# Score matmuls over 64 and over 128 rows: zeros under the lo queries

## The chip, the cores and the metric

The kernel runs on one core of one Trainium2 chip. The metric is the device time of one execution in microseconds. Before the change it is 826.6 us, the median of three runs (825.56 to 832.39).

## The reference, cut to what matters

A trunk of two decoder layers over 512 tokens of width 1024, in float32. Layer 0 is a recurrent time mixing (RWKV-7), layer 1 a causal differential attention over keys and values that are projected once from the result of layer 0. Only the attention touches the change:

```python
s = jnp.einsum('bhcqd,bhckd->bhcqk', q_blk.astype(f32), kf)     # 8 heads, 2 maps, 64 dims a map
s = jnp.where(k_pos[None, :] <= q_pos[:, None], s, -1e30)
prob = jax.nn.softmax(s, axis=-1)
attn = prob[:, :, 0] - lam * prob[:, :, 1]
return jnp.einsum('bhqk,bhkv->bhqv', attn, vf)
```

Each head has two maps (c = 0, 1) with queries and keys of 64 dims of their own; the two softmaxes are subtracted and one product with the values follows. The result is normalised, gated, projected, normalised again and added to the residual, and each layer ends with a gated embedding of its own.

## The kernel before, in words

**Exact products from pairs.** A float32 operand is held as two float32r parts, hi and lo (lo is what hi leaves over). A product is the sum hi·hi + hi·lo + lo·hi. The dense layers do this with three matmuls in a row into one PSUM bank, written by the helper `mm3` (lines 284, 285, 286), each with 128 rows of contraction and mostly 512 columns.

**The scores.** A query or key of one map has only 64 dims, so hi and lo of the keys share one tile: `kF[hg, x]` (loaded in `keys_in`) has the hi dims in rows 0 to 63 and the lo dims in rows 64 to 127. The queries come as two tiles a unit (`queries`, lines 1683 to 1700): `qh` holds the hi queries twice, in both halves of the rows, so one matmul over 128 rows gives hi·hi + hi·lo (line 1730). `ql` holds the lo queries in rows 0 to 63 alone, and a second matmul over 64 rows against the upper half of the keys adds lo·hi to the same bank (line 1731). `MAPS` (line 1611) is the pair of slices 0:64 and 64:128.

**Units, heads, streams.** A unit is one half of the heads (`hg`, four heads) by one block of 128 queries (`qb`); there are eight, in the order hg 0 with qb 0 to 3, then hg 1. A unit with block qb sees (qb + 1) · 128 keys, so its scores are 128, 256, 384 or 512 columns wide. Two generators, `heads_(0)` and `heads_(1)` (lines 1702 to 1774), go through the units with two heads each. A head issues: four score matmuls (two maps, hi and lo; a *group* in what follows); mask and maximum of each map on VectorE (1735, 1739); exponentials with sums on ScalarE (1742); reciprocal, weight and difference of the maps on VectorE (1747, 1749, 1751); one transpose per key block on TensorE (1757); the copy out of PSUM on ScalarE (1762); the products with the values on TensorE (1766). `unit_end` (1776 to 1814) normalises, gates and transposes a finished unit and frees its query tiles; its power runs on GpSimd in the helper `rsqrt` (280).

**What fills the rest of the stage.** The projections of keys, values, queries and gate (`layer1_proj`) run on TensorE in between, as do the first ones of the output projection. The weights come in by SyncE's DMA queue and are split into hi and lo on ScalarE, VectorE and GpSimd (`w_split`, lines 303 to 326; 269, 317, 321, 323).

**The order.** The instruction order of TensorE, VectorE, ScalarE and GpSimd is fixed when the kernel is built. The class `Streams` (lines 59 to 177) is a planner: every stream of work is a generator that yields steps such as `"PE", 0.68` (engine and cost in us), and the planner always issues the step that can start first by its own clocks. A step whose name ends in "!" books its engine, but its own stream goes on without waiting for it. Tiles come from pools by count (`"take"`, `"free"`); `"R"` is the big ring of 42 tiles of 4 KB a row, and both query tiles come from it. `queries` asks for a unit's two tiles as soon as the unit two places earlier has begun. The planner books a pair of score matmuls at 2 · max(0.11, n / 2250) us for n columns. The queries are loaded by three DMAs a unit on ScalarE's queue: hi into both halves of `qh` (line 1696, twice) and lo into `ql` (line 1698), 256 KB each.

Of the kernel before, what the change touches and what calls it, by code (L numbers as in the profile page):

```python
# [8 lines left out]
F32 = mybir.dt.float32  # L9
F32R = mybir.dt.float32r  # L10
# [5 lines left out]
P = 128  # L16
# [185 lines left out]
def yoco_kernel(ctx: ExitStack, tc: tile.TileContext, I, out):  # L202
    nc = tc.nc
# [26 lines left out]
    def bank(tag):  # L230
        return T(pp, [P, 512], "p", bufs=8)

    def R(shape, dt=F32):
        return T(ring, shape, "R", dt, bufs=N_R)

    def HT(shape, dt=F32):
        return T(hp, shape, "H", dt, bufs=N_H)
# [1373 lines left out]
    MAPS = (slice(0, 64), slice(64, P))  # L1611
# [69 lines left out]
    Q_ = {}  # L1681

    def queries(hg):

        for e in range(4):
            yield "wait", ("b", hg, e)
        for qb in range(NB):
            n = units.index((hg, qb))
            if n >= 2:
                yield "wait", ("unit",) + units[n - 2]  # L1690
            yield "take", "R", 2
            qh, ql = Q_[hg, qb] = R([P, 8, P], F32R), R([P, 8, P], F32R)[MAPS[0]]
            hi, lo = (qkD["b"][hg, n, :, :, qb * P : (qb + 1) * P] for n in range(2))
            yield "ACT", 0.9
            for m in range(2):
                nc.scalar.dma_start(qh[MAPS[m]].bitcast(F32), hi)
            yield "ACT", 0.45
            nc.scalar.dma_start(ql.bitcast(F32), lo)
            yield "DMA", 2.5
            yield "set", ("q", hg, qb)  # L1700

    def heads_(par):
        yield "wait", ("lam",)
        for hg, qb in units:
            n = (qb + 1) * P
            if par == 0:
                yield "take", "pw", 1
                U_[hg, qb] = (bank("pw"), T(lp, [P, 4, 2], "rc", bufs=2), T(lp, [P, 4], "oss", bufs=2))
                yield "spawn", unit_end(hg, qb), UEP
                yield "set", ("unit", hg, qb)  # L1710
            yield "wait", ("unit", hg, qb)
            for tb in range(qb + 1):
                yield "wait", ("vT", hg, tb)
            yield "wait", ("q", hg, qb)
            po, rc, oss = U_[hg, qb]
            qh, ql = Q_[hg, qb]
            for x in (par, par + 2):
                yield "wait", ("k", hg, x)
                yield "take", "H", 2
                E = [HT([P, S]) for _ in range(2)]  # L1720
                mx = T(lp, [P, 2], "mx", bufs=4)
                sm = T(lp, [P, 2], "sm", bufs=4)
                c1 = T(lp, [P, 1], "c1", bufs=4)
                scs = []
                yield "take", "pw", 2
                for m in range(2):
                    s_ = bank("pw")
                    yield "PE", 2 * max(0.11, n / 2250)
                    kt = kF[hg, x][:, m, 0:n]
                    nc.tensor.matmul(s_[:, 0:n], qh[:, 2 * x + m, :], kt, start=True, stop=False)  # L1730
                    nc.tensor.matmul(s_[:, 0:n], ql[:, 2 * x + m, :], kt[MAPS[0]], start=False, stop=True)  # L1731
                    scs.append(s_)
                for m in range(2):
                    yield "DVE!" if m == 0 else "DVE", 0.1 + n / 960
                    nc.vector.tensor_tensor_reduce(  # L1735
                        scs[m][:, 0:n], scs[m][:, 0:n], cmask[:, S - n : S], 1.0, -3.0e38, ALU.add, ALU.max, mx[:, m : m + 1]
                    )
                yield "DVE", 0.08
                nc.vector.tensor_scalar(mx, mx, -0.125, None, ALU.mult)  # L1739
                for m in range(2):  # L1740
                    yield "ACT", 0.18 + n / 960
                    nc.scalar.activation(  # L1742
                        E[m][:, 0:n], scs[m][:, 0:n], AF.Exp, bias=mx[:, m : m + 1], scale=0.125, accum_out=sm[:, m : m + 1]
                    )
                    yield "free", "pw", 1
                yield "DVE", 0.1
                nc.vector.reciprocal(rc[:, x, :], sm)
                yield "DVE", 0.13
                nc.vector.scalar_tensor_tensor(c1, sm[:, 0:1], nlam, rc[:, x, 1:2], ALU.mult, ALU.mult)
                yield "DVE+", 0.13 + n / 960  # L1750
                nc.vector.scalar_tensor_tensor(E[0][:, 0:n], E[1][:, 0:n], c1, E[0][:, 0:n], ALU.mult, ALU.add)
                yield "free", "H", 1
                yield "take", "pw", 1
                pt = bank("pw")
                yield "PE", 0.11 * (qb + 1)
                for kb in range(qb + 1):
                    nc.tensor.transpose(pt[:, kb * P : (kb + 1) * P], E[0][:, kb * P : (kb + 1) * P], ident)  # L1757
                yield "free", "H", 1
                yield "take", "H", 1
                aT = HT([P, S])  # L1760
                yield "ACT", 0.06 + n / 1200
                nc.scalar.copy(aT[:, 0:n], pt[:, 0:n])
                yield "free", "pw", 1
                yield "PE", 0.22 * (qb + 1)
                for kb in range(qb + 1):
                    nc.tensor.matmul(  # L1766
                        po[:, x * P : (x + 1) * P],
                        aT[:, kb * P : (kb + 1) * P],
                        vT[hg, kb // 2][:, kb % 2, x * P : (x + 1) * P],
                        start=(kb == 0),  # L1770
                        stop=(kb == qb),
                    )
                yield "free", "H", 1
                yield "set", ("pv", hg, qb, x)

    def unit_end(hg, qb):
        po, rc, oss = U_[hg, qb]
        for x in range(4):
            yield "wait", ("pv", hg, qb, x)
            yield "take", "H", 1  # L1780
            junk = HT([P, P])
            yield "ACT", 0.37
            nc.scalar.activation(
                junk, po[:, x * P : (x + 1) * P], AF.Square, scale=rc[:, x, 0:1], accum_out=oss[:, x : x + 1]
            )
            yield "free", "H", 1
        r = yield from rsqrt(lp, oss, 1.0 / P, SUBLN_EPS, 4, "or")
        yield "DVE", 0.1
        nc.vector.tensor_mul(r, r, rc[:, :, 0])
        yield "wait", ("gT", hg, qb)  # L1790
        yield "take", "R", 1
        oF[qb, hg] = o = R([P, 2, 4, P], F32R)
        yield "take", "H", 1
        og = HT([P, S])
        g_ = gT[hg, qb // 2][:, qb % 2, :]
        yield "DVE", 1.1
        for x in range(4):
            xs = slice(x * P, (x + 1) * P)
            nc.vector.scalar_tensor_tensor(og[:, xs], po[:, xs], r[:, x : x + 1], g_[:, xs], ALU.mult, ALU.mult)
        yield "free", "pw", 1  # L1800
        yield "take", "pw", 1
        pt = bank("pw")
        yield "PE", 0.45
        for x in range(4):
            nc.tensor.transpose(pt[:, x * P : (x + 1) * P], og[:, x * P : (x + 1) * P], ident)
        yield "free", "H", 1
        pv = pt.rearrange("p (a b) -> p a b", b=P)
        yield "ACT", 0.57
        nc.scalar.activation(o[:, 0], pv, AF.Copy, scale=subl)
        yield "DVE", 0.66  # L1810
        nc.vector.scalar_tensor_tensor(o[:, 1], pv, subl, o[:, 0].bitcast(F32), ALU.mult, ALU.subtract)
        yield "free", "pw", 1
        yield "free", "R", 2
        yield "set", ("oF", qb, hg)
# [28 lines left out]
    for hg in range(2):  # L1843
        sc.add(keys_in(hg), QP)
        sc.add(queries(hg), QP)
    for par in range(2):
        sc.add(heads_(par), HDP[par])
# [114 lines left out]
```

## Time and profile before

| | |
|---|---|
| runs | 825.56, 826.6, 832.39 us (median 826.6) |
| profiled execution | 824.56 us, of which the span of the core is 822.8 us |
| mean granted TensorE clock | 0.988 |
| TensorE (PE) busy | 779.5 us, 95% |
| weight loads (PEld) busy | 609.9 us, 74% |
| VectorE (DVE) busy | 595.2 us, 72% |
| ScalarE (ACT) busy | 454.8 us, 55% |
| GpSimd (POOL) busy | 192.6 us, 23% |
| HBM traffic | 144.60 MB by DMA, 176 GB/s on average |

How to read the rows that follow. In a timeline a row is: start in us from the beginning of the span, duration, engine, line, operation, out <- in, and for a matmul the size of the weights (rows * columns), then the moving operand (rows x columns) and the count. Matmuls are pipelined and their ends are modelled, so two rows may overlap: the pace of TensorE is the distance from one start to the next. In a table of windows each engine has its busy time with the number of instructions behind it; then come the granted clock, the share of DMA and GB/s. In a row of groups, the busy time and the mean in ns stand ahead of the idle time before them and what ended it. In the rows of one line, durations are minimum, median and maximum in ns. ACTq and PEldq are the engines' sequencers, which issue DMAs and wait.

### The profile page before, as it was taken

The numbers are of one execution on the slowest core, as the hardware profiler recorded it, in microseconds if no ns is written. First come the engines' busy times: TensorE is split into PE (matmuls) and PEld (weight loads), VectorE is DVE, ScalarE is ACT, GpSimd is POOL, SyncE is SP. The second block draws the span as 40 slices with busy tenths as digits, with TensorE's granted clock in tenths as the row PEclk, the third lists the DMA queues.
The fourth block names the chain that finished last, engine by engine and source line by source line (L and its number), as shares of the span: only waits on it lengthen the run. The fifth ranks groups of instructions, "written<-read, shape, count | busy, mean of one in ns | idle before, by whom it ended". The sixth has DMA issues, their size and how long they took to land.

```text
span 822.8 us, 13858 instructions
## 1 busy us (share of the span) xinstructions
PE 779.5 (95%) x5016; PEld 609.9 (74%) x5016; DVE 595.2 (72%) x1354; ACT 454.8 (55%) x1082; POOL 192.6 (23%) x211
## 2 busy tenths in 40 slices
PE   6898899997899698999999999999999999999996
PEld 3676678775677477777788888877777877788885
DVE  2999999987779887779685764466665567744844
ACT  3789754768547475565445563335564556544431
POOL 3406414323315406785010110000000002100000
PEclk9999999999999879999999999999999999999999
DMA  8676569632336568474564334888560433224602
GB/s 314 217 256 256 192 218 315 223 98 90 122 116 248 202 230 277 157 233 138 193 203 166 130 129 151 303 261 224 184 190 4 129 89 104 77 63 167 230 27 103
DMA packets 65525, 144.60 MB, mean 176 GB/s; under 512 B 6448, under 2 KB 27184, under 8 KB 65456
## 3 DMA queue, kind: packets, MB, share of 16 engines
q1 hardware_dynamic: 42672, 108.06, 39.2%
q10 hardware_dynamic: 22784, 35.66, 12.6%
q8 instruction: 39, 0.64, 0.3%
q14 instruction: 30, 0.25, 0.1%
HBM read 105.94 MB, written 37.75 MB: 175 GB/s over the span
## 4 chain that ended last, share of the span: by engine, by line
PE 69%; DVE 16%; ACT 7%; DMA 5%; issue 2%; POOL 1%; SPq 0%; ACTq 0%; DVEq 0%; POOLq 0%
PE p L284 18%; PE p L286 17%; PE p L285 16%; PE p L1731 3%; PE p L1766 2%; PE p L1168 2%; PE p L1730 2%; DVE p L1034 2%; DMA R<-in_xT 2%; PE p L964 2%; DVE H L1031 1%; PE p L1181 1%; PE p L1757 1%; ACT R L269 1%; DMA RAW<-in_w_g 1%
## 5 line engine op out<-in xcount | busy, mean ns | idle before, releaser
L284 PE MATMUL p<-R,R 128*128 128x512 f32 x800 | 328.9, 411 | 8.0 <-ACT R L535 7.0
L285 PE MATMUL p<-R,R 128*128 128x512 f32 x800 | 313.9, 392 | 4.2 <-DVE R L537 4.2
L286 PE MATMUL p<-R,R 128*128 128x512 f32 x800 | 314.4, 393 | 0.0
L284 PEld LDWEIGHTS p<-R,R 128*128 128x128 f32 x800 | 151.1, 189 | 44.7 <-ACT R L535 8.8
L285 PEld LDWEIGHTS p<-R,R 128*128 128x128 f32 x800 | 151.4, 189 | 32.5 <-DVE R L537 6.2
L286 PEld LDWEIGHTS p<-R,R 128*128 128x128 f32 x800 | 150.8, 189 | 33.2 <-DVE R L1298 0.4
L317 POOL TENSOR_TENSOR R<-RAW,R 128x512 fp32r<-128x512 f32 x50 | 67.9, 1364 | 165.5 <-ACT R L269 96.0
L269 ACT CAST R<-RAW 128x512 fp32r<-128x512 f32 x107 | 63.9, 619 | 17.3 <-DMA RAW<-in_w_k 8.0
L317 DVE TENSOR_TENSOR R<-RAW,R 128x512 fp32r<-128x512 f32 x90 | 62.2, 704 | 13.9 <-ACT R L269 13.1
L323 DVE SCALAR_TENSOR_TENSOR R<-RAW,vec,R 128x512 fp32r<-128x512 f32 x64 | 46.5, 749 | 14.6 <-ACT R L321 14.2
L280 POOL TENSOR_TENSOR orr<-orm,half 128x4 f32<-128x4 f32 x8 | 8.9, 1109 | 203.3 <-DVE orm L278 181.6
L321 ACT ACTIVATE R<-RAW,vec 128x512 fp32r<-128x512 f32 x64 | 44.5, 720 | 15.4 <-DMA RAW<-in_b_w_in 7.8
L1735 DVE CUSTOM_DVE_ANT_0 p<-p,cmask 128x128 f32<-128x128 f32 (+3 forms) x64 | 31.8, 498 | 24.4 <-PE p L1731 21.5
L1742 ACT ACTIVATE H<-p,mx 128x128 f32<-128x128 f32 (+3 forms) x64 | 33.3, 525 | 22.5 <-DVE mx L1739 19.3
L1377 POOL TENSOR_TENSOR hr<-hm,half 128x1 f32<-128x1 f32 x16 | 10.4, 647 | 145.7 <-DVE hm L1375 145.7
L1034 DVE TENSOR_TENSOR p<-p,H 128x126 f32<-128x126 f32 (+22 forms) x124 | 32.6, 263 | 4.3
L1031 DVE TENSOR_TENSOR H<-p,R 128x126 f32<-128x126 f32 (+22 forms) x124 | 30.7, 248 | 1.1
L529 ACT ACTIVATE p<-R,omm 128x512 f32<-128x512 f32 x32 | 22.1, 693 | 13.0 <-DVE R L973 5.8
L1514 DVE SCALAR_TENSOR_TENSOR R<-H,R 128x512 f32<-128x512 f32 x16 | 11.1, 691 | 24.4 <-ACT H L1507 22.6
L1436 ACT COPY R<-p 128x512 f32<-128x512 f32 x16 | 9.4, 586 | 31.5 <-PE p L286 31.2
L1507 ACT ACTIVATE H<-p 128x512 f32<-128x512 f32 x16 | 9.5, 595 | 31.2 <-PE p L286 31.2
L1731 PE MATMUL p<-R,R 64*128 64x128 f32 (+3 forms) x64 | 26.3, 410 | 0.5 <-DMA R<-bD 0.5
(220 smaller groups left out, 1270.0 us busy)
## 6 DMA issues: line engine op xcount, KB each, us to landing
mD<-R ACTq DMA_DIRECT2D x32, 512.0 KB, 3.9
R<-mD SPq DMA_DIRECT2D x32, 512.0 KB, 5.6
RAW<-in_ple_gate SPq DMA_DIRECT2D x16, 512.0 KB, 3.8
RAW<-in_kv_w SPq DMA_DIRECT2D x16, 512.0 KB, 3.8
RAW<-in_b_w_in SPq DMA_DIRECT2D x16, 512.0 KB, 4.1
R<-bD ACTq DMA_DIRECT2D x24, 256.0 KB, 4.2
R<-in_x SPq DMA_DIRECT2D x8, 512.0 KB, 6.2
RAW<-in_w_r SPq DMA_DIRECT2D x8, 512.0 KB, 4.1
```

The costliest lines, as they stand in the source:

```text
L269: (nc.scalar.copy if sc.eng == "ACT" else ENG[sc.eng].tensor_copy)(dst, src)
L284: nc.tensor.matmul(ps, ah, bh, start=first, stop=False)
L285: nc.tensor.matmul(ps, ah, bl, start=False, stop=False)
L286: nc.tensor.matmul(ps, al, bh, start=False, stop=last)
L317: ENG[sc.eng].tensor_sub(lo, f, hi.bitcast(F32))
L321: nc.scalar.activation(hi, f, AF.Copy, scale=g)
L323: nc.vector.scalar_tensor_tensor(lo, f, g, hi.bitcast(F32), ALU.mult, ALU.subtract)
L1031: ve.tensor_mul(tmp[:, 0:m, 0:w], bc(xs[:, s_ : s_ + 1, 0:w], [P, m, w]), bc(nb[:, s_ + 1 : 32, s_ : s_ + 1], [P, m, w]))
L1034: ve.tensor_add(xs[:, s_ + 1 : 32, 0:w], xs[:, s_ + 1 : 32, 0:w], tmp[:, 0:m, 0:w])
L1731: nc.tensor.matmul(s_[:, 0:n], ql[:, 2 * x + m, :], kt[MAPS[0]], start=False, stop=True)
L1735: nc.vector.tensor_tensor_reduce(scs[m][:, 0:n], scs[m][:, 0:n], cmask[:, S - n : S], 1.0, -3.0e38, ALU.add, ALU.max, mx[:, m : m + 1])
L1742: nc.scalar.activation(E[m][:, 0:n], scs[m][:, 0:n], AF.Exp, bias=mx[:, m : m + 1], scale=0.125, accum_out=sm[:, m : m + 1])
```

## The change

`ql` keeps its whole tile instead of the upper half of it. Rows 64 to 127 are set to zero by one GpSimd memset a unit (64 rows of 8 · 128 words), which the planner books at 1.0 us as a step that its stream doesn't wait for, ahead of the loads. The lo load goes into rows 0 to 63 as before. The second score matmul takes all 128 rows of `ql` and of the keys; the lo keys in rows 64 to 127 meet zeros, so the sum is the same.

```diff
-            qh, ql = Q_[hg, qb] = R([P, 8, P], F32R), R([P, 8, P], F32R)[MAPS[0]]
+            qh, ql = Q_[hg, qb] = R([P, 8, P], F32R), R([P, 8, P], F32R)
+            yield "Pool!", 1.0
+            nc.gpsimd.memset(ql[MAPS[1]].bitcast(F32), 0.0)
             hi, lo = (qkD["b"][hg, n, :, :, qb * P : (qb + 1) * P] for n in range(2))
             yield "ACT", 0.9
             for m in range(2):
                 nc.scalar.dma_start(qh[MAPS[m]].bitcast(F32), hi)
             yield "ACT", 0.45
-            nc.scalar.dma_start(ql.bitcast(F32), lo)
+            nc.scalar.dma_start(ql[MAPS[0]].bitcast(F32), lo)
             yield "DMA", 2.5
             yield "set", ("q", hg, qb)
...
                     nc.tensor.matmul(s_[:, 0:n], qh[:, 2 * x + m, :], kt, start=True, stop=False)
-                    nc.tensor.matmul(s_[:, 0:n], ql[:, 2 * x + m, :], kt[MAPS[0]], start=False, stop=True)
+                    nc.tensor.matmul(s_[:, 0:n], ql[:, 2 * x + m, :], kt, start=False, stop=True)
```

## The prediction

> **What bounds the kernel now.** I read the page first (busy shares, the slices, the chain that ended last), then the windows around the attention stage, then the order of instructions on TensorE inside it.
>
> ```profile
> PE 69%; DVE 16%; ACT 7%; DMA 5%; issue 2%; POOL 1%; SPq 0%; ACTq 0%; DVEq 0%; POOLq 0%
> L285 PEld LDWEIGHTS p<-R,R 128*128 128x128 f32 x800 | 151.4, 189 | 32.5 <-DVE R L537 6.2
> ```
> ```profile
> 552.00:735.00 183.00, 182.53 (x872) 139.90 (x871) 115.64 (x366) 101.16 (x291) 15.29 (x13) 1.00 0.42 124
> 735.00:780.00 45.00, 45.00 (x216) 37.23 (x215) 28.31 (x47) 19.32 (x42) 2.61 (x4) 1.00 0.51 174
> L1730 PE MATMUL p<-R,R x64: 220/385/502, 552.2 to 721.8; 128*128 128x128 f32 x16, 128*128 128x256 f32 x16, 128*128 128x384 f32 x16, 128*128 128x512 f32 x16
> ```
>
> TensorE holds 69% of the chain that ended last. The score matmuls start between 552.2 and about 722 us (last row), and in the stage from 552 to 735 TensorE is busy 182.53 of 183.00 us (first pair of numbers), VectorE 115.64, ScalarE 101.16 and GpSimd 15.29. TensorE is saturated at a granted clock of 1.00, and it stays so in the next window too. So whatever TensorE time the scores lose should come off the end, unless an engine behind it cannot follow. But "busy" hides how well the matmuls are packed. For that one reads starts, not durations. First a group of the widest scores (512 keys):
>
> ```profile
> 706.31 0.83 PE L1766 MATMUL p<-R,H 128*128 128x128 f32 x6
> 706.90 0.47 PE L1730 MATMUL p<-R,R 128*128 128x512 f32 x1
> 707.30 0.50 PE L1731 MATMUL p<-R,R 64*128 64x512 f32 x1
> 707.73 0.50 PE L1730 MATMUL p<-R,R 128*128 128x512 f32 x1
> 708.16 0.50 PE L1731 MATMUL p<-R,R 64*128 64x512 f32 x1
> 708.59 0.50 PE L284 MATMUL p<-R,R 128*128 128x512 f32 x1
> 708.93 0.40 PE L285 MATMUL p<-R,R 128*128 128x512 f32 x1
> 709.16 0.40 PE L286 MATMUL p<-R,R 128*128 128x512 f32 x1
> ```
>
> L285 to L286, both 128 rows by 512 columns, start 0.23 us apart. L1730 (128 rows) and L1731 (64 rows) have the same 512 columns, yet every start is 0.43 after the one before. The step from the last L1731 into the dense L284 is 0.43 as well, and the step after it 0.34. Each change between 128 and 64 rows costs about 0.2 us in which nothing streams. L284 to L286 add into one bank just as L1730 and L1731 do, and change their weights each time, and pay nothing; what sets the scores apart is the row count.
>
> **The change part by part.** *The matmuls.* There are 64 score pairs, 16 of each width (128, 256, 384 and 512 keys), in 32 groups of two pairs, eight groups a width. After the change all four matmuls of a group have 128 rows. The price of a 128-row matmul: at 512 columns 0.23 us. At 128 columns this row of eight, in the recurrent layer, gives a measure:
>
> ```profile
> 330.16 1.16 PE L1181 MATMUL p<-R,R 128*128 128x128 f32 x8
> 331.15 0.60 PE L1129 MATMUL p<-ident,R 128*128 128x128 f32 x4
> ```
>
> 0.99 us for eight, 0.124 each. For 384 and 256 columns no 128-row row stands alone; the bounds are the column rate of the wide one (0.23 / 512 = 0.45 ns a column: 0.173 and 0.115, the latter held up at 0.124) and the straight line between 0.124 and 0.23 (0.195 and 0.159). I take the lower ones, since loads are hidden wherever the stream is longer than they are.
>
> Width 512, from the rows above: 706.90 to 708.93 is 2.03 us for four scores and the L284 behind them. After: five times 0.23, plus 0.08 because a wide matmul behind a short one takes 0.31 to the next start (661.85 to 662.16 below): 1.23. Saved 0.80. The other widths:
>
> ```profile
> 591.45 0.34 PE L1730 MATMUL p<-R,R 128*128 128x384 f32 x1
> ...
> 592.83 0.50 PE L284 MATMUL p<-R,R 128*128 128x512 f32 x1
> 593.16 0.39 PE L285 MATMUL p<-R,R 128*128 128x512 f32 x1
> ```
> ```profile
> 661.85 0.48 PE L284 MATMUL p<-R,R 128*128 128x512 f32 x1
> 662.16 0.39 PE L285 MATMUL p<-R,R 128*128 128x512 f32 x1
> ...
> 662.63 0.28 PE L1730 MATMUL p<-R,R 128*128 128x256 f32 x1
> ...
> 663.77 0.49 PE L1766 MATMUL p<-R,H 128*128 128x128 f32 x2
> 664.02 0.48 PE L284 MATMUL p<-R,R 128*128 128x512 f32 x1
> ```
> ```profile
> 561.20 0.31 PE L1730 MATMUL p<-R,R 128*128 128x128 f32 x1
> ...
> 562.19 0.50 PE L284 MATMUL p<-R,R 128*128 128x512 f32 x1
> 562.53 0.40 PE L285 MATMUL p<-R,R 128*128 128x512 f32 x1
> ```
>
> 384: 1.71 us up to L285, after 4 x 0.173 + 0.23 = 0.92, saved 0.79. 256: 1.39 up to L284, after 4 x 0.124 + 2 x 0.10 = 0.70 (six L1766 pass in 0.59 us at 706.31), saved 0.69. 128: 1.33 up to L285, after 4 x 0.124 + 0.31 = 0.81, saved 0.52. One group of each: 2.80; times eight: 22.4. Wide groups followed by transposes instead of L284 save some 0.1 less, so I take 22. The straight line for 256 and 384 would take 1.8 off (16 groups with four matmuls each, 0.022 and 0.035 more): 20. Narrow ones at the 0.10 of L1766, and no 0.08 for wide ones behind short ones, would bring it to 24.
>
> What is lost at a change of rows is 0.43 - 0.23 = 0.20 us by these rows, whatever it is made of. The Trainium skill (TensorEngine Tiling (Array Packing), Key Properties) says that a change of tiling mode drains TensorE; with the 128 cycles at 2.4 GHz that TensorE: Matmul & The Clock Gate gives for the drain that is an estimate of 0.05 us a change, under 7 us for 128 changes, and 818 us or more for the execution if the drain were all that goes. By the trace the loss is four times that, so more than the drain stands open now; that the rest could stay is the second rival.
>
> *The memset.* Eight on GpSimd, one a unit, 64 rows of 1024 words each.
>
> ```profile
> L602 POOL MEMSET R<- 64x512 f32 x2 | 1.0, 518 | 0.1
> L317 POOL TENSOR_TENSOR R<-RAW,R 128x512 fp32r<-128x512 f32 x50 | 67.9, 1364 | 165.5 <-ACT R L269 96.0 <-DVE R L269 29.4 <-issue 16.1
> L280 POOL TENSOR_TENSOR orr<-orm,half 128x4 f32<-128x4 f32 x8 | 8.9, 1109 | 203.3 <-DVE orm L278 181.6 <-DVE mx L1739 21.5
> L1696 ACTq DMA_DIRECT2D R<-bD x16: 519/612/810, 543.6 to 671.6; - x16
> L1698 ACTq DMA_DIRECT2D R<-bD x8: 519/560/737, 544.9 to 674.4; - x8
> L1730 PEldq EVENT_SEMAPHORE  x10: 51/51/3859, 548.1 to 702.3; - x10
> ```
>
> Twice L602's 518 ns is 1.04 us, 8.3 in all, on an engine with 15.29 us of work in 183. Behind it in GpSimd's queue stand the unit-end powers (L280) and the splits of the output weights, which themselves wait long for VectorE and ScalarE. Its cover is the load of the same queries: the last is issued at 674.4 and the scores of the last unit are those of width 512 shown above, around 706. So it costs nothing on the path; uncovered it would be 1.04 a unit. The first unit has the least cover (issue at 544.9, first scores 552.2), still 7 us. The lo load keeps its size and its place on ScalarE's queue. The first lo matmul of a unit now waits for GpSimd as well as for the load: at most one more wait instruction of 51 ns a unit, 0.4 us together, which I charge in full (bounds 0 and 0.4). The planner books GpSimd for 1.0 where it is idle, so I expect the order elsewhere unchanged: 0, with 2 us either way for a reshuffle (the size of the smaller steps in this sum, as no row shows one).
>
> *What is late next.* VectorE's 115.64 us now lie in 183 and would lie in about 161, 72%: not a bound by sum. By chain it is closer. The transposes (L1757) need the softmax of their own group:
>
> ```profile
> 576.05 0.48 DVE L1751 SCALAR_TENSOR_TENSOR H<-H,c,H 128x256 f32<-128x256 f32 x1
> 701.61 0.62 DVE L1751 SCALAR_TENSOR_TENSOR H<-H,c,H 128x384 f32<-128x384 f32 x1
> ```
> ```profile
> 576.74 0.38 PE L1757 MATMUL p<-ident,H 128*128 128x128 f32 x2
> 703.56 0.49 PE L1757 MATMUL p<-ident,H 128*128 128x128 f32 x3
> ```
>
> The first pair has 0.21 us to spare, the second 1.33. Softmax starts when the first half of a group is done and so moves up only about half as much as the transposes (0.4 of 0.8), and where the other stream's group lies in between the spare time shrinks by another 0.7. The spare time of 1.33 is about used up by both; a tight one turns into a wait of 0.2 to 0.9. Bounds: none, or 0.3 in each of the 32 (10 us). I take a third of them at about 0.25: 2.5 us.
>
> Sum for the profiled execution: 824.56 - 22 + 0.4 + 2.5 = 805.5. The page's span is 822.8; 1.8 lie around it and stay. The runs shown have their median at 826.6, 2.0 above the profiled one, their lowest at 825.56, 1.0 above; I put the forecast 1.0 above: **806.5 us**.
>
> **The rivals.** *Softmax takes over.* The 10 us bound above: the saved time comes back as waits of TensorE at L1757 and L1766. For it: the 0.21 us; against it: VectorE has over 60 us free in the stage, and dense matmuls are ordered between. 824.56 - 22 + 0.4 + 10 + 1 = 814.
>
> *The loads stay exposed.* If two scores in a row of the same rows could not overlap load and stream, the three wider sizes would each pay the 0.08 seen behind short matmuls: 96 x 0.08 = 7.7, so 22 - 7.7 = 14 saved, and 814 with the other terms. Against it: L285's loads take 189 ns in the records, and L285 to L286 still start 0.23 apart. The Trainium skill (TensorE: Matmul & The Clock Gate, Part 3) says that a load overlaps running matmuls only where the row groups differ, which would give this rival; the dense rows above disagree.
>
> *The rows are not the cause.* If the gap came from something that the two products share (the same moving keys twice in a row), nothing is saved: 824.56 + 0.4 + 1 = 826. Against it: the L284 behind a group pays too (0.34 to the next start instead of 0.23 or 0.31), and it shares no keys.
>
> *Slower: the zeros hold up ScalarE's queue.* If the lo load waited for the whole tile, it would stand on ScalarE's queue until the memset is done, and the exponentials behind it too. A memset behind an L280 (1.11) and two weight splits (L317, 1.36) ends 1.11 + 2.72 + 1.04 = 4.9 us after the tile is free; the two hi issues (L1696, 0.61) cover 1.2. That leaves 3.7 a unit, 30 for eight: 824.56 - 22 + 30 + 1 = 834. It decides from 22 / 8 = 2.75 a unit on. Against it: the zeros and the load touch different rows, and GpSimd is busy 8% of the stage.
>
> **How the numbers follow.** The forecast has 0.72, softmax 0.14, exposed loads 0.06, no cause 0.05, slower 0.03. The forecast's own range is 801 to 810 (24 saved and nothing given back; 20 saved and 5 given back). The range of 800 to 815 adds the two rivals at 814 and leaves out the last two. One per cent, 8.3 us, is about what a measurement of this kernel can tell from no change; the first three cases lie beyond it: faster 0.92, same 0.05, slower 0.03.
>
> **What would show it.** Right: L1731 reads 128*128; starts within a 512 group 0.23 apart, within a 384 group 0.17 to 0.20, within a 128 group 0.12; the L284 behind a wide group followed by L285 after 0.23 to 0.31; eight memsets near 1.04 us, with nobody waiting for them; the stage about 20 us shorter, the rest unchanged; TensorE's waits at L1757 and L1766 grown to some 2.5 us. Wrong: starts still 0.4 apart, a TensorE idle time above 5 us in the stage, ScalarE's queue waiting on GpSimd, or a clock below 1.00 there.

## The result and the profile after

The changed kernel takes 805.5 us (median, 803.59 to 806.13) against 826.78 us for the kernel before (825.56 to 832.39): the ratio is 0.9726, 95% interval 0.9678 to 0.9774. The profiled execution took 804.9 us, its span 803.1 (822.8 before). The order of the instructions on TensorE, VectorE, ScalarE and SyncE is the same in both programs; only GpSimd has eight memsets more, so the two traces can be laid over each other, and lines behind the memset have moved down by two (L1730 is now L1732, L1731 L1733, L1757 L1759, L1766 L1768).

Windows cut at two marks that every run has: the start of the first score matmul, and the start of the transposes that end the last unit. First the kernel before, then the changed one:

```profile
552.22:735.10 182.88, 182.41 (x872) 139.73 (x871) 115.64 (x366) 101.26 (x291) 15.29 (x13) 1.00 0.41 124
735.10:822.80 87.70, 79.97 (x370) 65.89 (x368) 48.16 (x82) 30.99 (x67) 4.81 (x8) 0.98 0.36 126
```
```profile
553.11:715.44 162.33, 160.47 (x871) 136.09 (x871) 112.59 (x366) 99.67 (x291) 20.02 (x18) 1.00 0.46 137
715.44:803.10 87.66, 79.97 (x370) 65.89 (x368) 48.18 (x82) 30.99 (x67) 4.94 (x8) 0.98 0.36 126
```

The stage is 20.55 us shorter, the tail behind it the same to 0.04. The start of the first score lies 0.89 later, in work that the change doesn't touch: 20.55 - 0.89 + 0.04 = 19.7, the difference of the spans. That start scatters between 552.0 and 556.4 in the profiles below, whose order up to it is the same, which is most of the scatter of the times. So the stage is the sharper measure, and I give it for each experiment.

The group of 512 columns that answers to the one shown of before, from the timeline of the changed kernel:

```profile
689.01 0.83 PE L1768 MATMUL p<-R,H 128*128 128x128 f32 x6
689.59 0.48 PE L1732 MATMUL p<-R,R 128*128 128x512 f32 x1
689.91 0.40 PE L1733 MATMUL p<-R,R 128*128 128x512 f32 x1
690.14 0.40 PE L1732 MATMUL p<-R,R 128*128 128x512 f32 x1
690.38 0.40 PE L1733 MATMUL p<-R,R 128*128 128x512 f32 x1
690.61 0.39 PE L284 MATMUL p<-R,R 128*128 128x512 f32 x1
690.84 0.39 PE L285 MATMUL p<-R,R 128*128 128x512 f32 x1
```

L1733 now reads 128*128, and the starts are 0.23 apart where they were 0.43; only the first, behind the short L1768, has 0.32. The L284 behind the group no longer pays (0.23 to L285 instead of 0.34). The same for 384, 256 and 128 columns:

```profile
587.05 0.34 PE L1732 MATMUL p<-R,R 128*128 128x384 f32 x1
...
587.77 0.39 PE L284 MATMUL p<-R,R 128*128 128x512 f32 x1
588.00 0.40 PE L285 MATMUL p<-R,R 128*128 128x512 f32 x1
```
```profile
651.52 0.28 PE L1732 MATMUL p<-R,R 128*128 128x256 f32 x1
...
651.98 0.39 PE L1768 MATMUL p<-R,H 128*128 128x128 f32 x2
652.12 0.48 PE L284 MATMUL p<-R,R 128*128 128x512 f32 x1
```
```profile
560.72 0.31 PE L1732 MATMUL p<-R,R 128*128 128x128 f32 x1
560.86 0.27 PE L1733 MATMUL p<-R,R 128*128 128x128 f32 x1
560.97 0.27 PE L1732 MATMUL p<-R,R 128*128 128x128 f32 x1
...
561.48 0.39 PE L285 MATMUL p<-R,R 128*128 128x512 f32 x1
```

Up to the same marks as before: 1.25 us at 512 (was 2.03), 0.95 at 384 (1.71), 0.60 at 256 (1.39), 0.76 at 128 (1.33). For each of the four changes of rows in a group that is 0.20, 0.19, 0.20 and 0.14 us.

The weight loads of the same two groups of 512 columns show where the time went, first before, then after:

```profile
707.30 0.18 PEld L1731 LDWEIGHTS p<-R,R 64*128 64x128 f32 x1 [0.24 <-issue]
707.73 0.19 PEld L1730 LDWEIGHTS p<-R,R 128*128 128x128 f32 x1 [0.25 <-issue]
```
```profile
689.91 0.19 PEld L1732 LDWEIGHTS p<-R,R 128*128 128x128 f32 x1
690.14 0.19 PEld L1733 LDWEIGHTS p<-R,R 128*128 128x128 f32 x1
```

In the kernel before, the load behind each change of rows starts together with its own matmul (707.30 and 707.73), after 0.24 us in which no load ran; in the trace this holds within 3 ns at all 128 changes of the stage. In the changed kernel the load starts with the matmul before (689.91 for the one at 690.14), and so is done when its own turn comes. What a change costs is therefore close to one weight load of 0.18 us that nothing covers. This is read from the times; what makes the load wait at a change of rows, no run here shows.

TensorE's idle time in the stage has grown from 182.88 - 182.41 = 0.47 to 162.33 - 160.47 = 1.86 us. What it waited for in the changed kernel (total, times, longest), the memsets, and the additional wait instruction:

```profile
PE p L1732 <- issue: 1.1, 1, 1.1
PE p L1759 <- DVE rc L1749: 0.8, 1, 0.8
PE p L1733 <- DMA R<-bD: 0.5, 1, 0.5
PE p L1768 <- ACT H L1764: 0.4, 1, 0.4
```
```profile
L1694 POOL MEMSET R<- x8: 947/950/951, 516.3 to 654.3; 64x1024 f32 x8
```
```profile
L1733 PEldq EVENT_SEMAPHORE  x8: 51/51/51, 553.8 to 686.0; - x8
```

The first row lies ahead of the first score; the third, the wait for the first unit's load, is 0.5 in the kernel before too; the second and fourth are waits for the softmax and for the copy behind it, which the kernel before doesn't have. In the record of the memsets' line nothing waits for them.

### The profile page after: what moved, and what is told of

The parts are those of the page before. It is cut to its first block, busy times and chain, and to the rows that moved or that the text cites. A ratio compares the mean times of both kernels' runs of the same rounds, so it can differ in the third digit from the quotient of the medians.

```text
span 803.1 us, 13885 instructions
## 1 busy us (share of the span) xinstructions
PE 757.5 (94%) x5016; PEld 605.5 (75%) x5016; DVE 590.5 (74%) x1354; ACT 453.2 (56%) x1082; POOL 200.2 (25%) x219
## 4 chain that ended last, share of the span: by engine, by line
PE 64%; DVE 17%; DMA 8%; ACT 6%; issue 3%; POOL 1%; SPq 1%; ACTq 0%; DVEq 0%; POOLq 0%
PE p L284 16%; PE p L286 15%; PE p L285 15%; PE p L1168 2%; PE p L964 2%; PE p L1768 2%; DMA RAW<-in_b_w_in 2%; DVE p L1034 2%; DVE H L1031 1%; DVE R L317 1%; PE p L1181 1%; ACT R L269 1%; DMA R<-bD 1%; PE p L1733 1%; PE p L1732 1%
## 5 line engine op out<-in xcount | busy, mean ns | idle before, releaser
L284 PE MATMUL p<-R,R 128*128 128x512 f32 x800 | 327.4, 409 | 8.4 <-ACT R L535 7.4
L285 PE MATMUL p<-R,R 128*128 128x512 f32 x800 | 314.0, 393 | 4.1 <-DVE R L537 4.1
L284 PEld LDWEIGHTS p<-R,R 128*128 128x128 f32 x800 | 151.2, 189 | 42.3 <-ACT R L535 9.3
L285 PEld LDWEIGHTS p<-R,R 128*128 128x128 f32 x800 | 151.5, 189 | 32.8 <-DVE R L537 6.0
L321 ACT ACTIVATE R<-RAW,vec 128x512 fp32r<-128x512 f32 x64 | 44.6, 721 | 20.2 <-DMA RAW<-in_b_w_in 12.8
L1694 POOL MEMSET R<- 64x1024 f32 x8 | 7.6, 949 | 74.9 <-DMA kvD<-R 34.5
```

The costliest lines, as they stand in the source:

```text
L284: nc.tensor.matmul(ps, ah, bh, start=first, stop=False)
L285: nc.tensor.matmul(ps, ah, bl, start=False, stop=False)
L321: nc.scalar.activation(hi, f, AF.Copy, scale=g)
```

## Experiments

My theory: TensorE pays about 0.2 us at each change between 128 and 64 rows, and giving the lo products 128 rows removes all of these; the zeros are hidden; the softmax chains have less to spare than before. The rivals have a run each, but for the exposed loads, which the rows of the changed kernel answer.

**The zeros alone.**

```diff
-  matmul(s_[:, 0:n], ql[:, 2 * x + m, :], kt, ...)
+  matmul(s_[:, 0:n], ql[MAPS[0], 2 * x + m, :], kt[MAPS[0]], ...)
```

> The memset of the changed kernel alone; the lo products still take rows 0 to 63. My theory (the row count of the lo products brings the whole gain, the zeros are hidden on GpSimd): as before, 826.8 us within 2, score starts at width 512 still 0.43 apart, eight memsets of 0.95 us that nobody waits for. Rival (the zeros cost something that the gain covers up, through GpSimd's queue or the extra wait): 829 or more. Rival (the gain came from another order of the work, which the planner's new step brought): near 806 with starts unchanged.

Measured: 827.29 us, ratio to the kernel before 1.001 (0.9987 to 1.0034). The stage of that run:

```profile
554.13:736.96 182.83, 182.53 (x871) 139.90 (x871) 116.08 (x366) 101.30 (x291) 19.96 (x18) 1.00 0.41 124
```

182.83 against 182.88: the memset, the wait for it and the planner's new step together cost nothing that shows, and bring nothing, and the starts at 512 columns are still 0.43 apart. The whole gain is in the second matmul.

**Fewer changes of rows, same 64-row products.** In the kernel before, a group is issued as hi, hi, lo, lo:

```diff
+  for m in range(2):
+      matmul(scs[m][:, 0:n], qh[:, 2 * x + m, :], kts[m], start=True, stop=False)
+  for m in range(2):
+      matmul(scs[m][:, 0:n], ql[:, 2 * x + m, :], kts[m][MAPS[0]], start=False, stop=True)
```

> The kernel before, with the four products of a group in the order hi, hi, lo, lo instead of hi, lo, hi, lo; the lo products keep 64 rows. My theory (the price is paid at each change between 128 and 64 rows): two changes a group instead of four; at width 512 hi to hi and lo to lo start 0.23 apart, hi to lo and lo to the next 0.43; half of the 22 us saved, less some 1 us because the softmax of the first map starts later: 815 to 817. Rival (a 64-row product is slow by itself, and holds up what follows it): lo to lo starts 0.43 apart, only one of the four gaps goes: 821 to 822. Rival (the order matters, not the rows): no gap of 0.43 is left.

Measured: 814.62 us, ratio 0.985 (0.9818 to 0.9882). Its stage, a group of 512 columns (two equal products are merged into one row: L1731 is hi, L1733 lo), and the two lo products of that group alone, with the durations of each:

```profile
552.58:723.54 170.96, 170.73 (x871) 135.95 (x872) 112.62 (x366) 100.83 (x291) 15.32 (x13) 1.00 0.44 132
```
```profile
693.84 0.71 PE L1731 MATMUL p<-R,R 128*128 128x512 f32 x2
694.48 0.73 PE L1733 MATMUL p<-R,R 64*128 64x512 f32 x2
695.14 0.50 PE L284 MATMUL p<-R,R 128*128 128x512 f32 x1
695.48 0.39 PE L285 MATMUL p<-R,R 128*128 128x512 f32 x1
```
```profile
L1733 PE MATMUL p<-R,R x2: 393/443/493, 694.5 to 694.8; 64*128 64x512 f32 x2
```

The two lo products take 0.73 us together, and the second one's record is 0.39 long, so the second starts 0.34 behind the first, and L284 another 0.32 behind it. I had expected 0.23 and 0.43, and from hi to lo 0.43, where the trace has 0.33. No start-to-start gap of 0.43 is left in this group, which to the letter is what the third rival said. But starts mislead next to a change: the start of a matmul behind a change is that of its load too, as shown above, so a part of the price falls into the step before it and a part into the step behind it. L284 and L285, both of 128 rows, also start 0.34 apart here.

The sum is what counts: the group takes 1.64 us up to L285, halfway between 2.03 and 1.25: 0.39 for two changes, 0.20 each. The rival of the order would have 1.25. The first lo product up to L284 takes 0.66 us, which is 0.43 and 0.23: one price for two lo products, so the rival in which a 64-row product is slow by itself falls too. The stage is 11.9 us shorter than before, 0.58 of the 20.55; in busy time of TensorE it is 11.7 of 21.9, 0.53. The 814.6 us are just under the 815 to 817 that I expected.

**The order alone.** The same order in the changed kernel.

> The changed kernel with the order hi, hi, lo, lo. By my theory there is no change of rows left to save, so this is the control for the order alone: 805.5 us, up to 2 more because the mask of the first map starts one product later. If the order of the products had a price or gain of its own, it would show here.

Measured: 806.09 us, ratio 0.9752 (0.9721 to 0.9783).

```profile
555.29:717.95 162.66, 160.25 (x871) 136.04 (x870) 112.28 (x366) 99.45 (x291) 20.02 (x18) 1.00 0.46 139
```

0.33 us more in the stage than with the change: where no row count changes, the order of the four products has no gain of its own, which leaves nothing for the rival of the order, and the later start of the softmax costs little.

**Four times the zeros.**

```diff
+  for _ in range(4):
       nc.gpsimd.memset(ql[MAPS[1]].bitcast(F32), 0.0)
```

> The changed kernel with each memset done four times over: 3.8 us of GpSimd a unit instead of 0.95, with the order unchanged. My theory (the zeros have 7 us of cover or more in every unit): 805.5 us within 1.5. Rival (the cover is thin, through the powers of the unit ends behind the memsets or the first lo product of a unit): 3 us or more longer, with waits for GpSimd at the first lo product.

Measured: 805.7 us, ratio 0.9732 (0.9703 to 0.9762); the group of its memsets and its stage:

```profile
L1695 POOL MEMSET R<- 64x1024 f32 x32 | 30.3, 950 | 66.1 <-DMA kvD<-R 34.5 <-PE p L286 14.1 <-DVE mx L1742 11.7
```
```profile
552.02:714.01 161.99, 160.19 (x871) 135.94 (x870) 112.69 (x366) 99.73 (x291) 34.26 (x33) 1.00 0.47 140
```

Even 30.3 us of memset are covered; 7.6 are in the change.

**What stands in the rows.** Two runs: the lo queries loaded into both halves without any memset, and ones in place of the zeros.

```diff
-  nc.gpsimd.memset(ql[MAPS[1]].bitcast(F32), 0.0)
-  nc.scalar.dma_start(ql[MAPS[0]].bitcast(F32), lo)
+  for m in range(2):
+      nc.scalar.dma_start(ql[MAPS[m]].bitcast(F32), lo)
```

> The changed kernel without the memset: the lo queries are loaded into both halves by a second DMA of 256 KB a unit, so the second product adds lo times lo as well. My theory (128 rows are what counts, not what stands in them): 805.5 us within 2; eight more DMA issues of some 0.6 us on ScalarE's queue, which is idle over a third of the stage. Rival (zeros make the product cheaper, or eight more loads are in the way): 808 or more.

Measured: 811.25 us (806.78 to 814.01), ratio 0.9807 (0.9761 to 0.9853): slower than I expected, and in the rival's range. That left two causes, the values in the rows or the additional loads. The ones:

> The changed kernel with rows 64 to 127 of the lo queries set to one instead of zero, so each score has the sum of the lo keys added that the reference has not. My theory (only the number of rows counts, and the time that the run with the lo queries in both halves lost came from its eight additional loads): the stage and the time as with zeros, 805.5 us within 2. Rival (a product against values other than zero is slower): 810 or more.

Measured: 806.4 us, ratio 0.9753 (0.9695 to 0.981), with a stage of 162.86 us (shown below). So ones in place of zeros don't bring the loss. The loads alone, first by issuing the lo load twice into the same rows:

```diff
+  for _ in range(2):
       nc.scalar.dma_start(ql[MAPS[0]].bitcast(F32), lo)
```

> The changed kernel, zeros and all, with the lo load of each unit issued twice into the same rows: the eight additional loads alone. My theory: the loss of the run with the lo queries in both halves comes back here, 808 to 813 us, with TensorE waiting longer for the first unit's queries, since the DMA engines are busy there. Rival (the loads are hidden, it was what stood in the rows): 805.5 within 2.

Measured: 848.31 us, ratio 1.0264 (1.0209 to 1.032). This doesn't answer the question, but another one. The second load writes what the first writes, so it waits until the first has landed, and it waits on ScalarE's queue. ScalarE's timeline (the two issues, of 0.5 to 0.7 us each, take 8.62 us from first to last), who waited for the lo loads, and the stage:

```profile
548.51 8.62 ACTq L1701 DMA_DIRECT2D R<-bD  x2
557.18 0.72 ACT L321 ACTIVATE R<-RAW,vec 128x512 fp32r<-128x512 f32 x1 [9.74 <-DMA R<-bD]
```
```profile
  ACT R L321: 22.4, 3
  ACT H L1745: 19.6, 4
  ACT H L1786: 6.6, 1
  PE p L1734: 3.8, 1
```
```profile
556.06:759.05 202.99, 174.70 (x870) 146.48 (x871) 115.36 (x369) 101.37 (x294) 20.01 (x18) 0.92 0.40 124
```

It is the slower rival of the prediction with another cause in the place of the memset: the weight splits (L321) and the exponentials (L1745) stand still behind a load. It costs 848.31 - 805.5 = 43 us, 5.4 a unit. The stage has 40.7 of these, and only part of them is waiting: TensorE's idle time is 202.99 - 174.70 = 28.3 us instead of 1.9, 26.4 more. The other 14.2 are busy time at a granted clock of 0.92 instead of 1.00; 0.92 of 174.70 is about the busy time of the changed kernel (160.47). In the trace these are stretches of 3.4 to 10.2 us at half clock, which come with six of the eight waits of TensorE that are longer than 2 us.

The clean form sends the additional load to a buffer in HBM that nothing reads:

```diff
+  nc.scalar.dma_start(dumpD[n0], lo)
```

> The changed kernel with one more load a unit behind the lo load, of the same 256 KB, that goes to a buffer in HBM which nothing reads, so no load waits for another. My theory (the run with the lo queries in both halves lost its time to the eight additional loads): 808 to 812 us, with a stage some 2 to 3 us longer than with the change alone. Rival (the additional loads are hidden): 805.5 within 2, stage 162.

Measured: 807.12 us, ratio 0.9763 (0.9681 to 0.9846). And the lo queries in both halves beside it:

> The lo queries in both halves once more, beside the run with the spare load: 808 to 813 us if its loss is its own, 805 to 807 if the first runs of it were a matter of chance in the layer before.

Measured: 809.1 us, ratio 0.9789 (0.9714 to 0.9864). The stages: ones, spare load, then the two runs with the lo queries in both halves:

```profile
555.29:718.15 162.86, 160.49 (x870) 136.02 (x871) 112.92 (x366) 99.53 (x291) 20.04 (x18) 1.00 0.47 139
```
```profile
555.60:717.95 162.35, 160.46 (x870) 136.04 (x871) 111.70 (x366) 99.42 (x291) 20.04 (x18) 1.00 0.49 150
```
```profile
552.24:717.32 165.08, 160.40 (x872) 135.82 (x871) 111.76 (x366) 99.29 (x291) 15.34 (x13) 1.00 0.53 151
```
```profile
554.82:718.97 164.15, 160.57 (x871) 136.05 (x871) 111.64 (x366) 99.42 (x291) 15.34 (x13) 1.00 0.52 148
```

Eight additional loads for which nobody waits cost nothing in the stage (162.35), against my expectation; where the products wait for them the stage is 1.8 to 2.8 us longer, as idle time of TensorE (4.68 and 3.58 us instead of 1.86). One part is seen in the first of the two: the first lo product waits 1.8 us for its queries instead of 0.5.

```profile
PE p L1758 <- DVE rc L1748: 2.0, 2, 1.4
PE p L1732 <- DMA R<-bD: 1.8, 1, 1.8
```

So eight more loads as such don't bring the loss; that the product waits for one more load accounts for 1.3 us of it in the first run, and in the second, where this wait is 0.8 us, for 0.3. The softmax (L1758) is later too in both. At that place, around 645 us, the additional issue of 0.64 us stands between two exponentials on ScalarE, which idles for 0.84 us there and for 0.16 in the changed kernel; but the run with the spare load has the same 0.84, and TensorE waits no longer than with the change alone. Why the rest is lost, and why the times of these two runs scatter more than the stage explains, stays open.

**Is the spare time of the softmax smaller?** One more VectorE instruction in each of the 32 chains, in both kernels:

```diff
+  nc.vector.scalar_tensor_tensor(E[1][:, 0:n], E[1][:, 0:n], 0.0, E[1][:, 0:n], ALU.mult, ALU.add)
   nc.vector.scalar_tensor_tensor(E[0][:, 0:n], E[1][:, 0:n], c1, E[0][:, 0:n], ALU.mult, ALU.add)
```

> The kernel before, with one more VectorE instruction in each of the 32 softmax chains (the second map's exponentials times zero plus themselves, result unchanged): 0.35 to 0.75 us each, some 17.5 us of VectorE work in all. My theory (the chains have about 1.2 us to spare before the transposes here): most of it is hidden, 1 to 3 us longer, 828 to 830.

Measured: 827.96 us, ratio 1.0008 (0.9991 to 1.0025): nothing that shows, less than the 1 to 3 us I expected.

> The same extra instruction in the changed kernel. My theory (the shorter score groups have used up most of the spare time, and the 2 us given back are such waits): clearly more shows than in the kernel before, 5 to 8 us longer than the changed kernel, 811 to 814, and the waits stand at the transposes and the products with the values. Rival (the spare time is as it was, and the 2 us given back have another cause): the same 1 to 3 us as in the kernel before, 807 to 808.

Measured: 809.22 us, ratio 0.978 (0.9754 to 0.9807), 3.7 us above the change alone. The stages, before and changed, each with the addition:

```profile
556.42:741.25 184.83, 184.25 (x871) 141.11 (x871) 127.63 (x398) 101.15 (x291) 15.24 (x13) 0.99 0.41 121
```
```profile
553.18:718.72 165.54, 162.44 (x871) 135.42 (x870) 125.31 (x398) 100.47 (x291) 20.00 (x18) 1.00 0.46 137
```

VectorE has 12 to 13 us more to do in both. In the kernel before TensorE's idle time stays at 0.58 us (0.47 without); the stage's 1.95 us more are busy time at a granted clock of 0.99. In the changed kernel idle time grows from 1.86 to 3.10 and the stage by 3.2. The waits of the weight loads for the softmax result tell it more directly: the changed kernel, then with the addition:

```profile
PEld p L1759 <- DVE H L1753: 0.3, 1, 0.3
```
```profile
PEld p L1760 <- DVE H L1754: 3.4, 9, 0.6
```

What was wholly hidden now shows at nine of the chains, while the kernel before hides it: that much is the theory's, and speaks against a rival by which both kernels lose the same. The size is: 3.2 to 3.7 us lie outside both ranges, and closer to the rival's 1 to 3 than to my 5 to 8.

## Why the prediction was right

*The gain of the matmuls.* Forecast for one group of each width: 0.80, 0.79, 0.69 and 0.52 us; measured 0.78, 0.76, 0.79 and 0.57. The wide ones were right to 0.03. The narrow ones gain more, since a 128-row product of 128 columns starts 0.11 behind the last one, not 0.124, and one of 256 columns at the column rate. Times eight that is 23.2 instead of 22.4, inside the stated 20 to 24. For 256 and 384 columns the lower price was the right choice, but its reason was not: the loads of 0.19 us were to be hidden "wherever the stream is longer than they are", and the prices taken, 0.124 and 0.173, are shorter. The matmuls of 256 columns start 0.12 apart all the same. So that choice came out right by luck.

*Changes of rows are the cause.* Shown by the run with half of the changes. The Trainium skill (TensorEngine Tiling (Array Packing), Key Properties) says that changing the mode drains TensorE; the runs agree that a change is what costs, and give 0.20 us for it at 256 to 512 columns, four times what the drain alone was estimated at. By the traces nearly all of that is the weight load of 0.18 us, which at a change starts only with its own matmul. The prediction left open what the loss is made of. Behind a 64-row matmul the next one starts 0.25, 0.31, 0.37 and 0.43 us later at 128, 256, 384 and 512 columns (medians of the trace before): 0.46 ns a column, which is the pace of a wide matmul, and some 0.19 us that don't depend on the columns, by an estimate from these four. At 128 columns a change costs only 0.14, since there a matmul without a change already takes 0.11 us, more than the 0.06 of that pace a column.

*Loads exposed.* Didn't come: 0.23 from start to start at 512 columns, each load starting with the matmul before its own. The sentence of the Trainium skill (TensorE: Matmul & The Clock Gate, Part 3) by which loads overlap running matmuls only in other row groups does not hold in this kernel: score products now use all rows of the same groups one after the other at that pace.

*Memset and wait.* 0.95 us each instead of 1.04, and hidden. The wait instruction is there as forecast, eight of 51 ns, but the run with the zeros alone shows nothing on the path: of the 0.4 us charged none was due.

*Given back.* Forecast 2.5 us of new waits. TensorE's busy time in the stage fell by 182.41 - 160.47 = 21.94 us, where the sum has 22, and its idle time rose by 1.39: together the 20.55. So this term was put at nearly twice its size. That the new waits are for the softmax chains (0.8) and the copy behind them (0.4) is shown by the profile, and that the chains have less to spare by the added instruction; that they lost as much spare time as I worked out (0.4 of their own group and 0.7 of another) is not: the added instruction should then have cost more.

*The sum.* 805.5 us for the profiled execution against 804.9, and 806.5 for the median against 805.5. That it is so close is partly chance: the wait and the given-back time were put 1.5 us too high, and the first score happened to start 0.9 us later. The range of 801 to 810 lacks the 1.0 that was put on top for the median; with it, 24 saved and nothing given back would be 802, and 20 saved and 5 given back 811.

*The slower rival.* The lo load doesn't wait for the memset here. The price of such a wait was put at 3.7 us a unit; the double load, which did block ScalarE's queue, cost 5.4, of which 3.3 are waits of TensorE and most of the rest the lower clock.

## What to carry to other kernels

Where products over 64 and over 128 rows alternate on TensorE, count the changes, and read the time between two marks around a group, not busy time: here each cost 0.20 us at 256 to 512 columns, nearly as much as a whole matmul of 512 columns (0.23), and 0.14 at 128. Filling the short operand up with zeros on an idle engine removes all those of the scores, grouping equal row counts about half. Before adding a load to a queue that also feeds an engine, look at what it has to wait for: one that waits holds up everything behind it.

## What had not been expected of the hardware

A change of rows shows on both sides of the matmul behind it, and in both directions alike. In the run with hi, hi, lo, lo, the step into the 64-row pair is 0.33 us at 512 columns and the step behind the first lo product 0.34, instead of 0.23 each; the step out of the pair is 0.32 and the one from L284 to L285 0.34. So each change takes 0.09 or 0.10 ahead of the start that stands in the trace and 0.10 or 0.11 behind it, 0.20 in all. A single gap read from starts would have given half the price; only where a change follows each matmul, as in the kernel before, does the whole of it fall into one gap (0.43).

Waiting has a second price. In the run with the lo load issued twice, TensorE's granted clock in the stage fell to 0.92, and a third of the 40.7 us that the stage lost is matmuls at the lower clock, not waiting.
